# Masked softmax on one core: batch 5 and batch 0 exchange their places in the order of work

## The chip, the core and the metric

The kernel runs on one core of a Trainium2 chip. The metric is the device time of one execution in microseconds (us). Three executions of the kernel before took 156.1, 156.47 and 156.1 us, so the median is 156.1 us.

## What is computed

The input `x` holds 16 batches of 8 heads, each 256 by 256 in float32, and `lengths` holds one length for each batch. In every row only the first `length` columns count: they go through a softmax, and the other columns of the output are zero.

```python
for b in range(batch):
    length = lengths[b]
    masked = x[b, :, :, :length].copy()
    masked = masked - np.max(masked, axis=-1, keepdims=True)
    exp_masked = np.exp(masked)
    result[b, :, :, :length] = exp_masked / np.sum(exp_masked, axis=-1, keepdims=True)
```

The inputs come from a fixed draw. The lengths of batches 0 to 15 are 188, 233, 229, 243, 195, 252, 165, 210, 222, 180, 209, 157, 159, 199, 214 and 248.

## The kernel before, in words

One batch is a tile of 128 partitions by 16 rows by 256 columns, 2 MiB. The buffer `xt` has eight slots of that size, and the batch at position p of the order of work lies in slot p % 8. Before the change position p holds batch p. In what follows L4 is the load at position 4, S4 the store at position 4, and so on.

**Loads.** The first four positions are loaded whole (all 256 columns) by SyncE's queue, lines 128 to 132, the first of them in two halves. The other twelve come from GpSimd's queue, in the loop at line 178. For each it reads the length and takes the branch of `pick` (line 146) whose width is the smallest of 160, 168, ..., 240, 256 that holds the length; the DMA at line 152 then moves only so many columns of each row. The slots that are first filled in this way were set to zero beyond column 160 beforehand (line 174). In the pass for position p the loop waits until L(p-2) has landed (line 183), and until S(p-8) has landed where a slot is used again (line 184). So at most two of these loads are under way. The chip works on two DMA queues at once: q1 holds all that SyncE issues (the first loads, and every store), q0 holds GpSimd's loads.

**Stores.** SyncE issues them in the order of positions (lines 134 to 143), always whole rows, since the output has zeros beyond the length. Store 0 goes in one piece, positions 1 to 7 in a half and two quarters (called a, b and c below), 8 to 12 and 15 in two halves, 13 and 14 in one piece. Each piece waits until its division is done (line 138), and the first piece of S(p) also until S(p-2) has landed (line 140).

**Compute.** VectorE clips the right half of a batch to its length (line 222: `mask`), ScalarE takes the exponentials with the row sums (line 329), in two halves of a batch, and VectorE takes reciprocals and multiplies, half by half (lines 243 and 246: `divide`). From position 4 on VectorE's order is: first half of `divide(p)`, `mask(p + 1)`, second half of `divide(p)`. Ahead of that, `mask(4)` stands before both halves of `divide(3)`. A `mask` waits for its load. Behind the last division a few small instructions look whether a plain softmax with the row maximum would have to be done again; it is not done for this input.

Of the kernel before, what the change touches and what calls it, by code (L numbers as in the profile page):

```python
# [17 lines left out]
POOL = mybir.EngineType.Pool  # L18
# [3 lines left out]
def kernel(  # L22
# [6 lines left out]
    nc = tc.nc  # L29
    P = nc.NUM_PARTITIONS  # L30

    batch, heads, seq_q, seq_k = x.shape
# [6 lines left out]
    x_f = x.rearrange("b h q k -> b (h q) k").rearrange("b (p t) k -> b p t k", p=P)  # L39
    out_f = out.rearrange("b h q k -> b (h q) k").rearrange("b (p t) k -> b p t k", p=P)  # L40

    slots = 8
    ahead = 4
    assert slots - ahead == 4 and batch % slots == 0

    widths = list(range(160, 248, 8))
    low = widths[0]
# [3 lines left out]
    def parts(b):  # L51


        if b == 0:
            cuts = [0, nt]
        elif b < 8:
            cuts = [0, half, half + quarter, nt]
        elif b < 13 or b == batch - 1:
            cuts = [0, half, nt]
        else:  # L60
            cuts = [0, nt]
        return [slice(i, j) for i, j in zip(cuts, cuts[1:])]
# [3 lines left out]
    xt = pool.tile([P, slots, nt, seq_k], F32, name="xt")  # L66
    word64 = pool.tile([1, batch], mybir.dt.int64, name="word64")
    word = word64.bitcast(I32)
# [3 lines left out]
    len_s = pool.tile([P, batch], F32, name="len_s")  # L72
# [20 lines left out]
    with tc.tile_critical(no_gpsimd_drain=True):  # L93
# [4 lines left out]
        s_ld = [sem(f"s_ld{k}") for k in range(ahead + 1)]  # L98
# [19 lines left out]
        def length(engine, at):  # L118

            return nc.values_load(  # L120
                at,
                engines=[engine],
                skip_runtime_bounds_check_because="compared with constants, never an address",
            )
# [2 lines left out]
        nc.scalar.dma_start(out=word64, in_=lengths[None, :]).then_inc(s_word, 16)  # L127
        for h in range(2):
            s = slice(h * half, (h + 1) * half)
            nc.sync.dma_start(out=xt[:, 0, s], in_=x_f[0, :, s]).then_inc(s_ld[h], 16)  # L130
        for b in range(1, ahead):
            nc.sync.dma_start(out=xt[:, b], in_=x_f[b]).then_inc(s_ld[b + 1], 16)  # L132

        nc.sync.wait_ge(s_exp, 3)
        for b in range(batch):
            s_b = s_st[b % 2]
            for s in parts(b):
                nc.sync.wait_ge(s_out, 2 * b + (s.stop - 1) // half + 1)
                if b >= 2 and s.start == 0:
                    nc.sync.wait_ge(s_b, 64 * (b // 2 + 1))  # L140
                nc.sync.dma_start(  # L141
                    out=out_f[b, :, s, :], in_=xt[:, b % slots, s, :]
                ).then_inc(s_b, 16 * ((s.stop - s.start) // quarter))
        nc.sync.wait_ge(s_st[0], 64 * (batch // 2 + 1))

        def pick(v, n, slot, par, ws):

            if len(ws) == 1:  # L150
                w = ws[0]
                nc.gpsimd.dma_start(  # L152
                    out=xt[:, slot, :, :w], in_=x_n[:, n, :, :w]
                ).then_inc(s_sw[par], 16)
                return
            m = (len(ws) - 1) // 2
            with nc.gpsimd.If(v <= ws[m]):  # L157
                pick(v, n, slot, par, ws[: m + 1])
            with nc.gpsimd.Else():
                pick(v, n, slot, par, ws[m + 1 :])  # L160

        x_n = x_f.rearrange("b p t c -> p b t c")
        x_g = x_f.rearrange("b p t c -> p b (t c)")
# [14 lines left out]
        with nc.Fori(0, (batch - ahead) // 2, 1, engines=[POOL]) as q:  # L178
            for par in range(2):
                n = 2 * q + (ahead + par)  # L180
                v_len = length(POOL, word[0:1, bass.ds(2 * n, 1)])
                with nc.gpsimd.If(q >= 1):
                    nc.gpsimd.wait_ge(s_sw[par], 16 * q)
                    nc.gpsimd.wait_ge(s_st[par], 64 * q)
                pick(v_len, bass.ds(n, 1), bass.ds(n % slots, 1), par, widths + [seq_k])


        nc.tensor.wait_ge(s_ones, 2)
# [6 lines left out]
        v = 0  # L195

        def step(ins):
# [8 lines left out]
                out=down, in0=iota_i, scalar1=0.5, scalar2=-big, op0=ALU.add, op1=ALU.mult  # L206
# [7 lines left out]
                out=len_s, in0=len_f, scalar1=big, scalar2=None, op0=ALU.mult  # L214
# [4 lines left out]
        def clip(b, s, lo, hi):  # L219

            t = xt[:, b % slots, s, lo:hi]
            return nc.vector.scalar_tensor_tensor(  # L222
                out=t,
                in0=down[:, None, lo:hi].to_broadcast([P, s.stop - s.start, hi - lo]),
                scalar=len_s[:, b : b + 1],
                in1=t,
                op0=ALU.add,
                op1=ALU.min,
            )

        def mask(b, s):
            if b == 0:
                nc.vector.wait_ge(s_ld[s.start // half], 16)
            elif b < ahead:
                nc.vector.wait_ge(s_ld[b + 1], 16)
            else:
                nc.vector.wait_ge(s_sw[b % 2], 16 * ((b - ahead) // 2 + 1))
            clip(b, s, mid, seq_k).then_inc(s_min, 1)
# [41 lines left out]
        for k, (_, _, edge, op) in enumerate(checks):  # L280
            nc.vector.tensor_scalar(  # L281
                out=bad[:, k : k + 1],
# [13 lines left out]
        with nc.vector.Else():  # L296
            with nc.Fori(0, batch, 1, engines=[DVE]) as i:
                nc.vector.wait_ge(g_ld, 16 * i + 16)
                nc.vector.scalar_tensor_tensor(
                    out=g_t,  # L300
                    in0=down[:, None, :].to_broadcast([P, nt, seq_k]),
                    scalar=len_s[:, bass.ds(i, 1)],
# [6 lines left out]
                    out=neg_max, in_=g_t, op=ALU.max, axis=AX, negate=True  # L309
# [5 lines left out]
                    out=g_t,  # L315
# [25 lines left out]
        with nc.scalar.If(a_redo >= 1):  # L341
            for par in range(2):
                nc.scalar.wait_ge(s_st[par], 64 * (batch // 2 + 1))
            with nc.Fori(0, batch, 1, engines=[ACT]) as i:
                nc.scalar.dma_start(out=g_t, in_=x_g[:, bass.ds(i, 1)]).then_inc(g_ld, 16)
                nc.scalar.wait_ge(g_v, 3 * i + 2)
                with nc.Fori(0, nt, 1, engines=[ACT]) as t:
                    e = g_t[:, bass.ds(t, 1), :]
                    nc.scalar.activation(
                        out=e,  # L350
                        in_=e,
# [41 lines left out]
```

## Time and profile before

| what | value |
|---|---|
| median of the runs | 156.1 us |
| the profiled execution | 156.7 us, of which the span below is 155.1 us |
| VectorE busy | 117.0 us, 75% of the span |
| ScalarE busy | 105.2 us, 68% |
| GpSimd busy | 19.1 us, 12% |
| TensorE busy | 0.3 us |
| moved by DMA | 62.09 MB, mean 400 GB/s |
| queue q1 (SyncE's loads and all stores) | 41.95 MB, 65.7% of the time of 16 DMA engines |
| queue q0 (GpSimd's loads) | 20.12 MB, 32.0% of it |

The profile shows one execution. The span is what the profiler covers of it; 1.6 us of the execution lie around it. Times inside the span are counted from its start. There are 16 DMA engines, each working on packets from both queues; a share of 1 means that all 16 are busy. An engine's "idle before" names what the idle time ended with.

### The profile page before, as it was taken

Reading aid. Unit: us, or ns where it says so; the run is one execution under the profiler, and the core shown is the slowest. Engines: PE = TensorE matmul, PEld = TensorE weight load, DVE = VectorE, ACT = ScalarE, POOL = GpSimd, SP = SyncE. Lnnn points to the kernel's source line nnn. Section 1 sums busy time; section 2 is a strip of 40 time slices with the busy share of each in tenths; the row PEclk is TensorE's granted clock in tenths of the full one; section 3 lists DMA queues with packets and bytes.
Section 4 is the critical chain, followed back from the end, with each engine's and each line's share of the span. In section 5 each row is a group of like instructions: output and inputs, shape, how many; then the busy total and the mean of one; then the engine's idle time right before and its main releaser. Section 6 shows DMA issues by size and latency. Waiting matters only on the chain.

```text
span 155.1 us, 1298 instructions
## 1 busy us (share of the span) xinstructions
PE 0.3 (0%) x2; PEld 0.2 (0%) x2; DVE 117.0 (75%) x91; ACT 105.2 (68%) x514; POOL 19.1 (12%) x26
## 2 busy tenths in 40 slices
PE   0000000000000000000000000000000000000000
PEld 0000000000000000000000000000000000000000
DVE  1349999953999696969889696969679629796810
ACT  3096799992692959688795949595966906959200
POOL 4910031000220110202020020202001000000000
DMA  4999999999999999999999999999999999999991
GB/s 118 425 446 427 431 363 421 400 408 443 411 405 392 413 411 419 412 418 411 401 424 404 418 410 410 409 419 417 418 417 419 419 443 427 418 444 427 423 423 53
DMA packets 9989, 62.09 MB, mean 400 GB/s; under 512 B 850, under 2 KB 946, under 8 KB 6274
## 3 DMA queue, kind: packets, MB, share of 16 engines
q1 hardware_dynamic: 5904, 41.95, 65.7%
q0 software_dynamic: 4080, 20.12, 32.0%
q14 instruction: 3, 0.02, 0.0%
q10 hardware_dynamic: 2, 0.00, 0.0%
HBM read 28.51 MB, written 33.55 MB: 400 GB/s over the span
## 4 chain that ended last, share of the span: by engine, by line
DMA 55%; DVE 22%; ACT 7%; issue 6%; ACTq 2%; SPq 1%; POOLq 1%; PE 0%
DMA xt<-in_x_dram 34%; DMA out_dram<-xt 21%; DVE xt L246 12%; DVE xt L222 9%; ACT xt L329 7%; ACTq L329 2%; DVE inv_sum L243 1%; SPq L130 1%; DVE ends L278 0%; SPq L141 0%; POOLq L120 0%; ACTq L335 0%; SPq L132 0%; POOLq L157 0%; POOLq L152 0%
## 5 line engine op out<-in xcount | busy, mean ns | idle before, releaser
L329 ACT ACTIVATE xt<-xt (+1 forms) x256 | 102.3, 401 | 37.5 <-DVE xt L222 37.5
L246 DVE TENSOR_TENSOR xt<-xt,inv_sum 128x2048 f32<-128x2048 f32 x32 | 73.4, 2292 | 1.1
L222 DVE SCALAR_TENSOR_TENSOR xt<-down,len_s,xt 128x2048 f32<-128x2048 f32 (+1 forms) x17 | 37.8, 2222 | 13.4 <-DMA xt<-in_x_dram 13.2
L329 ACT ACTIVATION_READ_ACCUMULATOR xt<-xt (+1 forms) x256 | 47.8, 187 | 0.0
L152 POOL DMA_DIRECT2D xt<-in_x_dram x12 | 12.8, 1066 | 96.0 <-DMA out_dram<-xt 58.9
L243 DVE RECIPROCAL inv_sum<-row_sum 128x8 f32<-128x8 f32 x32 | 6.4, 199 | 14.3 <-ACT xt L329 14.3
L174 POOL MEMSET xt<- 128x1536 f32 x4 | 5.3, 1392 | 1.1 <-DVE len_s L213 1.1
L322 ACT ACT_TABLE_LOAD x1 | 1.3, 1283 | 1.6 <-SPq L93 1.6
L205 DVE TENSOR_SCALAR down<-iota_i 128x256 f32<-128x256 int32 x1 | 0.3, 302 | 1.6 <-POOL iota_i L165 1.6
L278 DVE TENSOR_REDUCE ends<-row_sum 128x1 f32<-128x256 f32 x2 | 0.7, 409 | 0.0
L192 PE MATMUL count<-bad,ones_c 128*1 128x3 bf16 x1 | 0.2, 165 | 145.2 <-DVE bad L281 145.2
L210 DVE CAST len_b<-word 1x16 bf16<-1x16 int32 x1 | 0.2, 162 | 0.4 <-DMA word<-in_lengths_dram 0.4
L213 DVE TENSOR_SCALAR len_s<-len_f 128x16 f32<-128x16 f32 x1 | 0.2, 175 | 0.4 <-PE len_f L190 0.4
L165 POOL IOTA iota_i<- 128x256 int32 x1 | 0.3, 332 | 0.6 <-SPq L93 0.6
L289 DVE TENSOR_REDUCE redo<-count 1x1 f32<-1x3 f32 x1 | 0.1, 148 | 0.3 <-PE count L192 0.3
L281 DVE TENSOR_SCALAR bad<-ends 128x1 bf16<-128x1 f32 x3 | 0.3, 150 | 0.0
L171 POOL MEMSET seed<- 1x1 f32 x2 | 0.2, 228 | 0.0
L192 PEld LDWEIGHTS count<-bad,ones_c 128*1 128x1 bf16 x1 | 0.1, 79 | 145.3 <-DVE bad L281 145.3
L322 ACT ACTIVATE warm<-const-float32-0.0 128x1 f32<-128x1 f32 x1 | 0.2, 203 | 0.0
L168 POOL MEMSET ones<- 1x128 bf16 x1 | 0.2, 195 | 0.0
L190 PE MATMUL len_f<-len_b,ones 1*128 1x16 bf16 x1 | 0.2, 168 | 2.6 <-DVE len_b L210 2.6
L278 DVE TENSOR_REDUCE ends<-len_s 128x1 f32<-128x16 f32 x1 | 0.2, 158 | 0.0
(7 smaller groups left out, 0.6 us busy)
## 6 DMA issues: line engine op xcount, KB each, us to landing
out_dram<-xt SPq DMA_DIRECT2D x19, 1024.0 KB
out_dram<-xt SPq DMA_DIRECT2D x14, 512.0 KB
xt<-in_x_dram SPq DMA_DIRECT2D x3, 2048.0 KB, 16.2
out_dram<-xt SPq DMA_DIRECT2D x3, 2048.0 KB
xt<-in_x_dram POOLq DMA_DIRECT2D x3, 1728.0 KB, 16.8
xt<-in_x_dram POOLq DMA_DIRECT2D x2, 2048.0 KB, 18.5
xt<-in_x_dram POOLq DMA_DIRECT2D x2, 1600.0 KB, 17.0
xt<-in_x_dram POOLq DMA_DIRECT2D x2, 1280.0 KB, 15.0
```

The source lines that it names most:

```text
L130: nc.sync.dma_start(out=xt[:, 0, s], in_=x_f[0, :, s]).then_inc(s_ld[h], 16)
L152: nc.gpsimd.dma_start(out=xt[:, slot, :, :w], in_=x_n[:, n, :, :w]).then_inc(s_sw[par], 16)
L165: nc.gpsimd.iota(iota_i, pattern=[[1, seq_k]], base=0, channel_multiplier=0).then_inc(s_iota, 1)
L174: nc.gpsimd.memset(xt[:, b, :, low:], 0.0).then_inc(s_fill, 1)
L192: nc.tensor.matmul(count, lhsT=ones_c, rhs=bad, start=True, stop=True).then_inc(s_count, 1)
L205: nc.vector.tensor_scalar(out=down, in0=iota_i, scalar1=0.5, scalar2=-big, op0=ALU.add, op1=ALU.mult)
L222: return nc.vector.scalar_tensor_tensor(out=t, in0=down[:, None, lo:hi].to_broadcast([P, s.stop - s.start, hi - lo]), scalar=len_s[:, b : ...
L243: step(nc.vector.reciprocal(out=inv_sum[:, b, s], in_=row_sum[:, b, s]))
L246: nc.vector.tensor_tensor(out=t, in0=t, in1=inv_sum[:, b, s, None].to_broadcast([P, half, seq_k]), op=ALU.mult,).then_inc(s_out, 1)
L278: step(nc.vector.tensor_reduce(out=ends[:, k : k + 1], in_=values, op=op, axis=AX))
L322: nc.scalar.activation(out=warm, in_=nc.const_aps.tensor(0.0, (P, 1), F32), func=EXP)
L329: ins = nc.scalar.activation(out=e, in_=e, func=EXP, accum_out=sum_h[:, i, j])
```

## The change

A table `batch_of` says which batch stands at a position: batch 5 at position 0, batch 0 at position 5, every other batch at its own number. Position 0 is loaded whole by SyncE, as before, but with the data of batch 5. Position 5 is loaded by GpSimd, as before, but with batch 0, whose width is 192 where that of batch 5 was 256. The stores go to the addresses of the batches at their positions and keep their sizes, since these go by the position. In GpSimd's loop the batch number for the odd positions is computed in registers: q = 0 gives batch 0, later q give 2q + 5. `mask` takes the length of the batch at its position; slots, semaphores and the order of the engines' instructions are as before.

```diff
+    def batch_of(pos):
+        return {0: 5, 5: 0}.get(pos, pos)
...
-            nc.sync.dma_start(out=xt[:, 0, s], in_=x_f[0, :, s]).then_inc(s_ld[h], 16)
+            nc.sync.dma_start(out=xt[:, 0, s], in_=x_f[batch_of(0), :, s]).then_inc(s_ld[h], 16)
         for b in range(1, ahead):
-            nc.sync.dma_start(out=xt[:, b], in_=x_f[b]).then_inc(s_ld[b + 1], 16)
+            nc.sync.dma_start(out=xt[:, b], in_=x_f[batch_of(b)]).then_inc(s_ld[b + 1], 16)
...
-                    out=out_f[b, :, s, :], in_=xt[:, b % slots, s, :]
+                    out=out_f[batch_of(b), :, s, :], in_=xt[:, b % slots, s, :]
...
                 n = 2 * q + (ahead + par)
-                v_len = length(POOL, word[0:1, bass.ds(2 * n, 1)])
+                b = 2 * q + (q + 7) // 8 * 5 if par else n
+                v_len = length(POOL, word[0:1, bass.ds(2 * b, 1)])
                 with nc.gpsimd.If(q >= 1):
                     nc.gpsimd.wait_ge(s_sw[par], 16 * q)
                     nc.gpsimd.wait_ge(s_st[par], 64 * q)
-                pick(v_len, bass.ds(n, 1), bass.ds(n % slots, 1), par, widths + [seq_k])
+                pick(v_len, bass.ds(b, 1), bass.ds(n % slots, 1), par, widths + [seq_k])
...
-                scalar=len_s[:, b : b + 1],
+                scalar=len_s[:, batch_of(b) : batch_of(b) + 1],
```

More of the change, by code (lines that the diff above doesn't have):

```diff
@@ L43 @@
     ahead = 4
-    assert slots - ahead == 4 and batch % slots == 0
+    assert slots - ahead == 4 and batch == 2 * slots
+    def batch_of(pos):
+        return {0: 5, 5: 0}.get(pos, pos)
     widths = list(range(160, 248, 8))
@@ L141, with pick @@
                 nc.sync.dma_start(
-                    out=out_f[b, :, s, :], in_=xt[:, b % slots, s, :]
+                    out=out_f[batch_of(b), :, s, :], in_=xt[:, b % slots, s, :]
                 ).then_inc(s_b, 16 * ((s.stop - s.start) // quarter))
         nc.sync.wait_ge(s_st[0], 64 * (batch // 2 + 1))
-        def pick(v, n, slot, par, ws):
+        def pick(v, b, slot, par, ws):
             if len(ws) == 1:
@@ L152, in pick @@
                 nc.gpsimd.dma_start(
-                    out=xt[:, slot, :, :w], in_=x_n[:, n, :, :w]
+                    out=xt[:, slot, :, :w], in_=x_n[:, b, :, :w]
                 ).then_inc(s_sw[par], 16)
@@ L157, in pick @@
             with nc.gpsimd.If(v <= ws[m]):
-                pick(v, n, slot, par, ws[: m + 1])
+                pick(v, b, slot, par, ws[: m + 1])
             with nc.gpsimd.Else():
-                pick(v, n, slot, par, ws[m + 1 :])
+                pick(v, b, slot, par, ws[m + 1 :])
         x_n = x_f.rearrange("b p t c -> p b t c")
```

## Prediction

> **What bounds the kernel now.** I read the page's slices first, then the stretches, then the order in time of VectorE, GpSimd and SyncE, and last the trace's single DMA packets.
>
> The slices: the DMA engines are full from the second slice to the last but one, no compute engine is.
>
> ```profile
> DVE  1349999953999696969889696969679629796810
> ACT  3096799992692959688795949595966906959200
> ...
> DMA  4999999999999999999999999999999999999991
> ```
>
> The stretches (start:end, length, busy time of PE, PEld, DVE, ACT, POOL with counts, clock, DMA share, GB/s) say the same near the end:
>
> ```profile
> 127.00:140.00 13.00, 0.00 (x0) 0.00 (x0) 11.75 (x8) 8.63 (x43) 0.00 (x0) 1.00 1.02 432
> 140.00:147.30 7.30, 0.00 (x0) 0.00 (x0) 5.41 (x7) 4.37 (x22) 0.00 (x0) 1.00 0.99 421
> 147.30:152.00 4.70, 0.17 (x1) 0.08 (x1) 0.78 (x6) 0.00 (x0) 0.00 (x0) 1.00 0.90 382
> ```
>
> So bytes bound it, but a second limit lies close by. VectorE in order of time (start, length; idle before it in brackets):
>
> ```profile
> 115.16 2.35 DVE L222 SCALAR_TENSOR_TENSOR xt<-down,len_s,xt 128x2048 f32<-128x2048 f32 x1 [0.89 <-DMA xt<-in_x_dram]
> ...
> 126.88 2.35 DVE L222 SCALAR_TENSOR_TENSOR xt<-down,len_s,xt 128x2048 f32<-128x2048 f32 x1 [3.25 <-DMA xt<-in_x_dram]
> ...
> 137.76 2.29 DVE L246 TENSOR_TENSOR xt<-xt,inv_sum 128x2048 f32<-128x2048 f32 x1
> ```
>
> mask(13) and mask(14) wait for their loads. From mask(14) at 126.88 to the end of the second half of divide(14), 137.76 + 2.29 = 140.05, nothing waits for a DMA: 13.2 us of compute hang on L14. SyncE issues S14 at 140.08, at once. Behind it come 2 + 1 + 1 MiB. By the packet records the slowest of the 16 engines ends the last store at 153.4; S14 and S15 are 8 packets of 16 KB and 16 of 8 KB for it, 8 x 0.613 + 16 x 0.317 = 10.0 us at the records' mean durations, so it was free for S14 at 143.4. So S14 comes about 2 us before the slowest engine needs it. **If L14 lands over 2 us later, that engine idles, and the end moves.**
>
> **How the two queues share.** Counted from the packet records, per DMA engine: every whole or part store is 8 packets (of 16, 8 or 4 KB, for whole, half, quarter); a whole load is 8 of 16 KB; a narrow load is cut into packets of several rows, under 5 KB: 22 for width 200, 19 for 168, 26 for 216. With both queues filled the engines alternate: from 104 to 112 us 272 packets of 4800 B (q0) and 244 of 8 KB (q1), from 116 to 124 288 of 4320 B and 257, from 36 to 40 87 of 16 KB and 90 of 4 KB. q0 gets 1.0 to 1.15 packets per store packet whatever their sizes. The Trainium skill (DMA: Bandwidth & Descriptors, Queues, rings and completion order) says that an engine goes round its queues packet by packet; the counts agree. Beside quarters (4 KB) a whole load thus takes four fifths of the bandwidth; a narrow one takes little over half, and beside halves (8 KB) two fifths.
>
> **The change part by part.**
>
> 1. *Bytes.* Position 0 stays 2 MiB. L5 goes from 8 x 16 KB packets per engine, 613 ns each: 4.90 us, to 128 rows of 768 B per engine; six to a packet as for 736 and 800 B rows, so 21 of 4608 B and a short one. Between 177 ns (4416 B) and 191 (4800 B) I take 184: 21 x 0.184 + 0.06 = 3.92 us. **-0.98 us** of all engines. The bounds are -0.8 and -1.1 (22 x 0.191, and 21 x 0.177 + 0.06). The Trainium skill (same page, Anatomy of one DMA) prices moving data at bytes / 436e9; for 0.524 MB that is an estimate of 1.20 us. By it the term would be -1.2; the rows decide.
>
> 2. *Registers.* GpSimd gets one extra register operation for each odd length and one in each odd branch. Its register rows are 29 ns (move) and 110 to 130 (fused). The length is read before the waits, so hidden; the one in the branch costs odd loads 0 to 0.13 us at issue. Writing L5's descriptors takes about 1.15 us in place of 0.56:
>
> ```profile
> 20.93 1.30 POOL L152 DMA_DIRECT2D xt<-in_x_dram  x1 [12.53 <-issue]
> 24.14 0.56 POOL L152 DMA_DIRECT2D xt<-in_x_dram  x1 [1.92 <-issue]
> 38.80 1.16 POOL L152 DMA_DIRECT2D xt<-in_x_dram  x1 [14.10 <-issue]
> 44.98 1.15 POOL L152 DMA_DIRECT2D xt<-in_x_dram  x1 [5.02 <-DMA out_dram<-xt]
> ```
>
> L4 keeps q0 filled to 36.3, so this costs 0 (0.6 without that cover). The addresses of S0 and S5 and the scalars of two masks change, no size: 0.
>
> 3. *L5 gets slower though smaller.* Before, its 8 packets per engine met 8 store packets (S1c): 36.3 to 42.2, landed 43.55. Now 22 packets meet about 20: 8 of S1c, 8 of S2a (8 KB), 4 of S2b. A q0 packet with a 4 KB partner takes 0.32 (4320 B) to 0.36 us (4800 B), with an 8 KB one 0.44 to 0.47; 13 x 0.34 + 9 x 0.46 = 8.5 us. It lands at about 46.0, **2.5 us later**; mask(5) started at 47.04 without waiting, so 1 us remains there.
>
> 4. *The gate of L7.* L6 was issued at 38.80, 1.4 us after L4 landed (37.43), and its first packets came at 43.5, 4.7 us behind the issue; from 42.2 to 43.5 and more q0 was empty and some 4 store packets per engine ran alone. Now L5 covers that. But L7 waits for L5: 46.0 + 1.4 + 4.7 = 52.1 for its first packet, up to 52.9, where it was 50.5 to 51.3: +1.6, with some 0.1 of point 2; I take **+1.8**. Behind this wait on GpSimd stands only the pass of L8, issued at 53.58 before and gated by L6. The engines do not idle, so what L7 loses the stores gain: (1.8 + 0.98) / 0.317 us (an 8 KB packet) = 9 store packets ahead.
>
> 5. *It stays.* Thereafter the queues alternate as before, and stores have slack to run ahead: the second half of divide(8) is done at 85.35, S8 moves from 97. So L10 (landed 89.01, S7a next) still sees stores 8 x 0.317 + 0.2 = 2.7 ahead, less 0.98: +1.7. L12 is gated by L10: issued at 90.52, first packets 95.2, when L11 had ended at 94.5: so +1.7 there too. From there L12, L13, L14 have 19, 22 and 26 packets, now all beside 8 KB pieces: 19 x 0.4475 + 22 x 0.47 + 26 x 0.444 = 30.4 us, before 29.7 (95.2 to the ends around 124.9), because L12 had 4 KB partners at first: +0.7. **L14 lands 2.4 us later**, at about 129.2. Bounds: 0.3 if the stores ahead at the time of L10 are 4 KB ones, 4.0 if q0 gets no more than one packet per store packet and a new hole opens at L12.
>
> 6. *The tail.* S14 is issued at 140.08 + 2.4 = 142.5. From issue to first packet the trace has 1.0 us (first load, 1.14 to 2.15) and 2.5 (S13, 134.17 to 136.7, behind others); nearer the empty queue I take 1.5, so 144.0. The slowest engine is free at 143.4 - 0.98 = 142.4. It idles 1.6 us: the end moves by -0.98 + 1.6 = **+0.6 us**. S15's halves (issued 144.11 and 146.95, so 149.4 and first packets by 150.9) then come behind 144.0 + 4.9 + 2.5 = 151.4 and are hidden. Against the profiled execution's own 156.7 that is 157.3; the runs' median is 0.6 below that execution, so **156.7 us**.
>
> In short: end = the larger of -0.98 (bytes bind) and L14's delay minus 1.8 (compute after L14 binds).
>
> **Rivals.**
>
> *The bytes win.* If L14 is late by under 0.8 us, all -0.98 is kept: 155.1; up to 1.3, some of it: 155.6. For it: full DMA in all slices, and q0 drawing more than one packet per store packet; stores that get ahead may run dry at S12 or S13, which wait for their division, and then q0 has the engines alone. Against it: S8 to S11 have 10 us and more of such slack, and the gates of L7 and L12 do not depend on bytes.
>
> *They cancel.* L14 late by 1.3 to 2.3: within 0.5 us of 156.1, 0.3%, about what a measurement of this kernel can tell from no change.
>
> *The loads fall further behind* (slower still). With one to one, 22 packets meet 22, and if L6 ends before L7's gate and L11 before L12's by more, 3 to 5 more store packets go first (0.317 each): L14 +3.4 to 4.0, end +1.6 to 2.2: 157.7 to 158.3. It decides from 2.3 us of delay on, the forecast being its mild form.
>
> *The change does not do what it says*: batch 0 falls in another branch than 192. Then q0 would not drop by 0.52 MB; with 256 columns the time stays at 156.1.
>
> **How the numbers follow.** Forecast (L14 late by 2.3 to 3.3, +0.5 to +1.5): 0.39. Further behind: 0.09. Cancel: 0.22, and 0.02 for a change that does nothing. Bytes win: 0.28. So slower by over 0.3% 0.48, within 0.24, faster 0.28. The range from 155.1 (bytes alone) to 157.8 leaves out the last of "further behind" and what is faster than the bytes: about 2 in 10.
>
> **What would show it.** Right: moved bytes 61.57 MB; L5 lands near 46 and not at 43.5; L7 issued near 47.5 (44.98 before); mask(14) starts near 129 after a wait over 4 us; the DMA share dips below 0.95 between 140 and 145. Wrong: L5 lands at 43 or earlier (no alternation by packets); mask(14) at 127 or before (the lead of the stores was lost again); no dip in the tail although mask(14) is late (more slack there than 1.8 us).

## The result, and the profile after

The changed kernel takes 157.91 us (median of six executions, 157.38 to 158.78); the kernel before, run beside it, 156.25 us (155.68 to 156.59). The ratio is 1.0111, with a 95% interval of 1.0074 to 1.0148: **slower by 1.1%, 1.66 us**. The prediction was slower too, but by 0.6 us, 156.7 us in a range up to 157.8; the time lies just outside. The profiled execution after took 157.94 us with a span of 156.3 us.

The slices of the page, as before the change:

```profile
DVE  1349999944999696877969677997966656697780
ACT  3096899991792959588494947869591970978800
...
DMA  4999999999999999999999999999999999992994
GB/s 115 428 438 436 432 361 415 406 406 415 393 380 412 398 419 410 414 419 406 418 403 416 415 409 418 411 417 419 415 416 419 418 437 423 409 455 109 419 403 203
DMA packets 10213, 61.57 MB, mean 394 GB/s; under 512 B 850, under 2 KB 962, under 8 KB 6626
```

0.52 MB less is moved, as the change says. But the row of the DMA engines has a hole in the fourth slice from the end, where it had none. The stretches around it (columns as in the prediction):

```profile
127.00:140.00 13.00, 0.00 (x0) 0.00 (x0) 8.52 (x7) 7.33 (x37) 0.00 (x0) 1.00 1.03 436
140.00:142.50 2.50, 0.00 (x0) 0.00 (x0) 2.46 (x3) 1.04 (x5) 0.00 (x0) 1.00 0.46 197
142.50:144.50 2.00, 0.00 (x0) 0.00 (x0) 1.14 (x1) 2.00 (x11) 0.00 (x0) 1.00 0.00 0
144.50:152.00 7.50, 0.17 (x1) 0.08 (x1) 6.15 (x11) 3.45 (x18) 0.00 (x0) 1.00 1.02 428
```

For two microseconds not one data packet starts. S13 has gone out, and S14 waits for the division. VectorE in order of time says why the division is late:

```profile
118.74 2.35 DVE L227 SCALAR_TENSOR_TENSOR xt<-down,len_s,xt 128x2048 f32<-128x2048 f32 x1 [1.50 <-DMA xt<-in_x_dram]
...
130.47 2.35 DVE L227 SCALAR_TENSOR_TENSOR xt<-down,len_s,xt 128x2048 f32<-128x2048 f32 x1 [3.26 <-DMA xt<-in_x_dram]
...
141.35 2.29 DVE L251 TENSOR_TENSOR xt<-xt,inv_sum 128x2048 f32<-128x2048 f32 x1
```

mask(14) starts at 130.47, 3.6 us later than before, because L14 lands so late. The 13.2 us of compute behind it are the same (141.35 + 2.29 = 143.64), S14 is issued at 143.67, and its first packet moves at 144.51. GpSimd's issues show where the lateness began:

```profile
24.53 1.15 POOL L156 DMA_DIRECT2D xt<-in_x_dram  x1 [2.36 <-issue]
38.82 1.15 POOL L156 DMA_DIRECT2D xt<-in_x_dram  x1 [13.13 <-issue]
47.61 1.15 POOL L156 DMA_DIRECT2D xt<-in_x_dram  x1 [7.64 <-issue]
```

L6 is issued when it was before, L5 0.4 us later but long before L4 ends (36.1); L7, which waits for L5, at 47.61 in place of 44.98, since L5 with fewer bytes landed at 46.10 in place of 43.55.

How far the stores get ahead can be counted in the packet records: store packets sent (q1, per engine, from the start, the first loads included) when the median engine ends or starts a load.

| when | before | after | ahead |
|---|---|---|---|
| L4 ends | 64.9 | 64.7 | 0 |
| L5 ends | 73.2 | 85.1 | 11.9 |
| L6 starts | 79.2 | 88.4 | 9.2 |
| L6 ends | 95.5 | 107.2 | 11.7 |
| L7 ends | 120.2 | 132.6 | 12.4 |
| L10 ends | 191.0 | 203.8 | 12.8 |
| L12 starts | 212.8 | 225.9 | 13.1 |
| L14 ends | 273.2 | 286.4 | 13.2 |

The stores win the lead beside L5 and L6 and keep it for 80 us.

### The profile page after: what moved, and what is told of

The parts are those of the page before. It is cut to its first block, busy times and chain, and to the rows that moved or that the text cites. A ratio compares the mean times of both kernels' runs of the same rounds, so it can differ in the third digit from the quotient of the medians.

```text
span 156.3 us, 1312 instructions
## 1 busy us (share of the span) xinstructions
PE 0.3 (0%) x2; PEld 0.2 (0%) x2; DVE 117.2 (75%) x91; ACT 105.2 (67%) x514; POOL 19.7 (13%) x26
## 4 chain that ended last, share of the span: by engine, by line
DMA 76%; DVE 7%; issue 6%; ACT 4%; POOLq 2%; ACTq 1%; SPq 1%; PE 0%
DMA xt<-in_x_dram 76%; ACT xt L334 4%; DVE xt L227 3%; DVE xt L251 3%; ACTq L334 1%; POOLq L161 1%; POOLq L156 1%; SPq L134 1%; DVE ends L283 0%; POOLq L124 0%; DVE inv_sum L248 0%; SPq L136 0%; DVE bad L286 0%; POOLq L187 0%; ACTq L340 0%
## 5 line engine op out<-in xcount | busy, mean ns | idle before, releaser
L156 POOL DMA_DIRECT2D xt<-in_x_dram x12 | 13.4, 1116 | 99.0 <-issue 99.0
```

The lines of the kernel that those rows point to most:

```text
L156: nc.gpsimd.dma_start(out=xt[:, slot, :, :w], in_=x_n[:, b, :, :w]).then_inc(s_sw[par], 16)
```

## The experiments

The theory: the DMA engines take turns between the queues packet by packet; 22 thin packets in L5's place let 13 more store packets pass before L14 is in, L14 is 3.6 us late, and S14 and what follows come after the engines have run dry. Rival A: something else of the change costs the time, the registers and longer descriptor writing on GpSimd, or the addresses. Rival B: bytes alone count, and the rest is scatter. Each kernel was timed beside the kernel before on the same chip, and each ratio is to those runs.

### The exchange without the narrow load, and a wider narrow load

In the first of two kernels position 5 is loaded whole. The number added to the length is 64 at position 5 and zero later.

```diff
+                if par:
+                    v_len = v_len + (1 - (q + 7) // 8) * 64
                 pick(v_len, bass.ds(b, 1), bass.ds(n % slots, 1), par, widths + [seq_k])
```

> The changed kernel, but position 5 (batch 0) is loaded with all 256 columns: 8 packets of 16 KB per DMA engine instead of 22 thin ones. The exchange, the registers and the addresses stay. Theory (the engines alternate packet by packet, so 22 thin packets let the stores get about 13 packets ahead, L14 comes late, and the tail idles): L5 lands near 43.5 us as before the change, mask(14) starts near 127, no idle in the tail, time about 156.2 us, ratio to before 1.000. Rival A (something else of the change costs it: GpSimd's registers and its longer descriptor writing, the other addresses): as the changed kernel, about 157.9. Rival B (bytes alone, the rest scatter): 156.2 too, so the next kernel is what tells B apart.

Measured: 156.12 us beside 156.08, ratio 1.0009 (0.9998 to 1.0021). The loss is gone. L5 lands at 43.31, mask(14) starts at 126.85, and the stretches of the tail are full:

```profile
126.85 2.35 DVE L229 SCALAR_TENSOR_TENSOR xt<-down,len_s,xt 128x2048 f32<-128x2048 f32 x1 [3.25 <-DMA xt<-in_x_dram]
...
140.00:142.50 2.50, 0.00 (x0) 0.00 (x0) 1.31 (x3) 2.50 (x13) 0.00 (x0) 1.00 1.00 426
142.50:144.50 2.00, 0.00 (x0) 0.00 (x0) 1.34 (x2) 1.83 (x10) 0.00 (x0) 1.00 1.01 434
```

The exchange, its registers and its addresses cost nothing that can be measured. With the whole width the writing of L5's descriptors is short again as well (0.56 us and not 1.15), so this run alone does not clear that part of rival A; the kernel with four loads under way, below, keeps the 1.15 us and takes 155.91 us. Rival A falls. In the second kernel the added number is 50, so batch 0 is loaded 240 columns wide: nearly the bytes of the kernel before, in 26 thin packets.

```diff
-                    v_len = v_len + (1 - (q + 7) // 8) * 64
+                    v_len = v_len + (1 - (q + 7) // 8) * 50
```

> The changed kernel, but position 5 is loaded 240 columns wide: 128 rows of 960 B per engine, 5 to a packet, 26 packets, 1.97 MB, 0.13 MB less than the kernel before moved. Theory: 4 packets more than in the changed kernel, so the stores get 16 to 17 packets ahead of where they are in the kernel before; L5's own work is 4.95 us as before, so L14 lands 16.5 x 0.317 = 5.2 us later than before (about 132), and the end follows with about 2.4 us of slack: +2.8 us, 159 us (158.3 to 160). Rival B (bytes): 156.1. Rival A (something else of the change): 157.9.

Measured: 159.11 us, ratio 1.0203 (1.018 to 1.0226). L5 lands at 47.79, 4.2 us later than before. VectorE's two waits late in the run, and the tail:

```profile
119.57 2.35 DVE L229 SCALAR_TENSOR_TENSOR xt<-down,len_s,xt 128x2048 f32<-128x2048 f32 x1 [1.41 <-DMA xt<-in_x_dram]
131.29 2.35 DVE L229 SCALAR_TENSOR_TENSOR xt<-down,len_s,xt 128x2048 f32<-128x2048 f32 x1 [3.26 <-DMA xt<-in_x_dram]
```

```profile
140.00:142.50 2.50, 0.00 (x0) 0.00 (x0) 2.47 (x3) 0.61 (x3) 0.00 (x0) 1.00 0.86 367
142.50:145.50 3.00, 0.00 (x0) 0.00 (x0) 1.97 (x1) 3.00 (x17) 0.00 (x0) 1.00 0.22 93
```

0.13 MB less than the kernel before, and 3 us slower: rival B falls. Loads of almost the same bytes differ by three microseconds by how they are cut. L14 was less late than expected (131.3, not 132): the lead at its end was 286.7 - 273.2 = 13.5 packets where 16 to 17 were expected. It was 137.9 - 120.2 = 17.7 at the end of L7 and shrank from there on. The packet records show where: between L9 and L10, and between L11 and L12, only about one store packet per engine passes here, where about 3 and 4 pass in the kernel before and in the changed kernel. No run tries why L10 and L12 follow so closely here.

### The tail

S14 goes out in two halves, the first of which waits only for the first half of its division.

```diff
-        elif b < 13 or b == batch - 1:
+        elif b != 13:
             cuts = [0, half, nt]
```

> The changed kernel, but S14 goes out in two halves, so its first half can be issued when the first half of divide(14) is done, near 139, and not at 143.7. Theory (the engines idle from 142.6 to 144.5 because S14 comes late): that idle time goes; then the halves of S15 bind, whose last is issued when all division is done (150.5) and needs 0.85 + 2.5 us: the end comes 0.6 to 0.9 us earlier than in the changed kernel, about 157.1 us. If the tail's idle time were not on the path: no change, 157.9.

Measured: 157.42 us, ratio 1.0088 (1.0066 to 1.011); 0.5 us less than the changed kernel, 157.91. But the interval of that one's ratio (1.0074 to 1.0148) holds this one's, so the gain is not shown. The hole did not close but was broken up: by the packet records the engines run low before each of the last stores (around 137, 145, 148.5 to 149, and 152). The stretch with one of these holes:

```profile
147.00:149.50 2.50, 0.00 (x0) 0.00 (x0) 1.81 (x3) 1.91 (x10) 0.00 (x0) 1.00 0.57 233
```

In this execution L14 also landed later than in the changed kernel (131.40 against 130.44), so the run does not single out the tail. It does show that S14 in one piece is not the whole of the loss: all that follows L14 is late, and the idle time comes back elsewhere.

### Three ways to bring the loads forward

If the lateness of L14 is the cause, whatever cures it must cure the time, at either end of the run. One: S8 to S12 in a half and two quarters, so the late loads meet 4 KB packets.

```diff
-        elif b < 8:
+        elif b < 13:
             cuts = [0, half, half + quarter, nt]
```

> The changed kernel, but S8 to S12 go out in a half and two quarters, like S1 to S7, so L12 to L14 meet 4 KB packets for two thirds of theirs. Theory: a thin load packet takes 0.32 to 0.36 us beside a 4 KB packet and 0.44 to 0.47 beside an 8 KB one, so L12 to L14 take about 25 us in place of 30; mask(14) no longer waits for its load or much less (start near 126 or before), the engines do not idle in the tail, and the end is set by the bytes: 0.98 us less than before plus some 0.2 us for more small packets, 155.4 us. Rivals A and B, in which the alternation plays no part: 157.9 to 158.1.

Measured: 156.56 us, ratio 1.0024 (1.0012 to 1.0036). mask(14) starts with no wait, and the engines' share stays at 0.94 to 1.03 from 140 to 150.5; the theory holds for that:

```profile
125.96 2.34 DVE L227 SCALAR_TENSOR_TENSOR xt<-down,len_s,xt 128x2048 f32<-128x2048 f32 x1
```

But the time is not the expected 155.4. The same edit in the kernel before is the control:

> The kernel before the change, with S8 to S12 in a half and two quarters: the control of the quarters. Its engines never idle, so loads that come earlier win nothing. Theory (the end is set by the packets' time): 640 store packets of 8 KB become 1280 of 4 KB, 640 x (2 x 163 - 317 ns) / 16 = +0.36 us, 156.4 us. The difference to the changed kernel with quarters (156.56) is then what the change is worth when the loads are not late: -0.98 us if only the bytes count (then this run would be at 157.5), near 0 if the engines' saving is used up by longer packets (156.4 to 156.6). Rival: quarters help the kernel before as well (155.5 or less).

Measured: 156.67 us, ratio 1.0036 (1.0025 to 1.0047). So the quarters cost 0.6 us by themselves (0.36%), where 0.36 us was expected and the packet records show 0.42 us more per engine (151.54 against 151.12), and with them the change is worth -0.1 to -0.2 us, which the two intervals do not tell from nothing. Two: the same quarters for S11 and S12 alone.

```diff
-        elif b < 8:
+        elif b < 8 or b in (11, 12):
```

> The changed kernel with only S11 and S12 in a half and two quarters. L14 meets S11a and then the two quarters of S11: 26 load packets take 8 x 0.444 + 18 x 0.32 = 9.3 us in place of 11.1. Theory: L14 lands near 128.6, the end comes 1.8 us earlier, 156.1 us, where the engines' packets bind (with 0.15 us for the small packets). If lateness of L14 were not what sets the end: 157.9 to 158.1.

Measured: 156.19 us, ratio 1.0013 (1.0001 to 1.0025). mask(14) starts at 127.85, after a wait of 1.35 us for its load; the time is the expected one. Three: S2 and S3 in four quarters, 80 us ahead of the tail, where the lead is won.

```diff
+        elif b in (2, 3):
+            cuts = [0, quarter, half, half + quarter, nt]
         elif b < 8:
```

> The changed kernel with S2 and S3 in four quarters each, so L5 and L6 meet only 4 KB packets: the stores get ahead by the same number of packets but by fewer bytes; 8 more packets of 4 KB in each of S2 and S3 hold the stores back by 2 x 8 x 0.163 = 2.6 us. Theory (the lead that the stores win beside L5 to L7 is what makes L14 late, at the other end of the run): L14 lands near 127.8 and the end comes 1.9 us earlier, at the limit of the engines' packets, 156.0 us. If the lead were lost or won again on the way, or L14's delay came from the late positions alone: 157.9 us.

Measured: 155.76 us, ratio 0.9981 (0.9967 to 0.9994). The only waits for loads late in the run:

```profile
114.40 2.35 DVE L229 SCALAR_TENSOR_TENSOR xt<-down,len_s,xt 128x2048 f32<-128x2048 f32 x1 [0.33 <-DMA xt<-in_x_dram]
126.09 2.35 DVE L229 SCALAR_TENSOR_TENSOR xt<-down,len_s,xt 128x2048 f32<-128x2048 f32 x1 [3.22 <-DMA xt<-in_x_dram]
```

An edit that touches two stores before 60 us moves mask(14) by 4.4 us and the end by 2.1 us (2.0 by the ratios): the lead is won early and carried through. At the end of L14 the stores are 289.5 - 273.2 = 16 packets ahead, and 16 is what the finer cut of S2 and S3 adds for the same bytes, so in bytes no lead is left. This kernel has the lowest median of the study. It beats the kernel before by 0.2%, barely clear of the noise, and its interval meets that of the kernel with four loads, below.

### The gates of the loads

Up to four of GpSimd's loads may be under way, with a semaphore for each position modulo 4.

```diff
-        with nc.Fori(0, (batch - ahead) // 2, 1, engines=[POOL]) as q:
-            for par in range(2):
-                n = 2 * q + (ahead + par)
-                b = 2 * q + (q + 7) // 8 * 5 if par else n
+        with nc.Fori(0, (batch - ahead) // 4, 1, engines=[POOL]) as r:
+            for j in range(4):
+                n = 4 * r + (ahead + j)
+                b = 4 * r + (r + 3) // 4 * 5 if j == 1 else n
...
-                with nc.gpsimd.If(q >= 1):
-                    nc.gpsimd.wait_ge(s_sw[par], 16 * q)
-                    nc.gpsimd.wait_ge(s_st[par], 64 * q)
+                with nc.gpsimd.If(r >= 1):
+                    nc.gpsimd.wait_ge(s_sw[j], 16 * r)
+                    nc.gpsimd.wait_ge(s_st[j % 2], 128 * r + 64 * (j // 2))
```

> The changed kernel, but up to four of GpSimd's loads may be under way (four semaphores for them, one per position modulo 4), so L(p) waits for L(p-4) and not L(p-2). Theory with the gates as a cause: in the changed kernel a DMA engine sends 1.9, 3.0 and 4.5 store packets alone between L6 and L7, L9 and L10, L11 and L12, where 1.2 is usual; these 5.8 packets x 0.317 = 1.8 us go, L14 lands near 128.6 and the end comes 1.8 us earlier, 156.1 us. If only the number of thin packets counts and the gates do not: 157.9 us.

Measured: 155.91 us, ratio 0.9992 (0.9981 to 1.0003). GpSimd issues L4 to L7 in one go:

```profile
20.83 1.31 POOL L156 DMA_DIRECT2D xt<-in_x_dram  x1 [12.44 <-issue]
24.51 1.15 POOL L156 DMA_DIRECT2D xt<-in_x_dram  x1 [2.38 <-issue]
27.13 1.15 POOL L156 DMA_DIRECT2D xt<-in_x_dram  x1 [1.47 <-issue]
30.33 1.15 POOL L156 DMA_DIRECT2D xt<-in_x_dram  x1 [2.05 <-issue]
```

L5 still takes until 44.55 (median engine) and gives the stores about the same lead (85.7 packets, 85.1 in the changed kernel); but from then on only 1.0 to 2.1 store packets pass between two loads, and at the end of L14 the lead is 275.2 - 273.2 = 2:

```profile
127.31 2.35 DVE L227 SCALAR_TENSOR_TENSOR xt<-down,len_s,xt 128x2048 f32<-128x2048 f32 x1 [3.25 <-DMA xt<-in_x_dram]
```

The thin packets make the lead, and loads that are queued ahead win it back. The kernel before was not run with four loads under way; it has holes between its loads too (6.0 store packets between L5 and L6, by the table), so it is not shown that the exchange costs nothing where both kernels have none.

### What the bytes are worth once the loads are on time

Two last kernels: the kernel before with S2 and S3 in quarters, and the changed kernel with both cures.

> The kernel before the change with S2 and S3 in four quarters each: the control of the run before last with these quarters (155.76 us). There the loads come early enough already, so theory says only the packets' time counts: 256 store packets of 8 KB become 512 of 4 KB, 256 x 9 ns / 16 = +0.14 us, 156.1 us. The changed kernel with the same quarters is then 0.35 us below it: what is left of the 0.98 us by which L5 got smaller. If the full 0.98 us were to be had, this run would be at 156.7; if the quarters themselves are what gained, at 155.6.

> The changed kernel with both cures: four loads under way, and S2 and S3 in four quarters. Theory: L14 lands near 124.5 and no longer matters, the engines never idle, and the end is the time of their packets, as with the quarters alone (155.76) or 0.2 us under it: 155.5 to 155.8 us. If L14 still set the end in the run with the quarters alone: 154.5 or less.

Measured: 156.53 us, ratio 1.0029 (1.0017 to 1.004), and 156.43 us, ratio 1.0018 (1.0004 to 1.0031). The first says that the quarters of S2 and S3 cost the kernel before 0.5 us, and that with them the change is worth 155.76 - 156.53 = -0.8 us (ratios 0.9981 and 1.0029, intervals apart), near the -0.98 of the bytes. The other pair of kernels, with S8 to S12 in quarters, gave only -0.1 to -0.2 us, so what the bytes are worth depends on the rest of the order and is not one number. The run with both cures does not fit: L14 lands at 121.84, the packets' time is the least of all (150.4 us per engine), and its median is still 0.7 us above that with the quarters alone. Its profiled execution took 155.76 us, the lowest of its twelve, so the trace does not hold the time that the median lost. The expectation for both was missed, and what sets the last half microsecond in kernels whose loads come very early stays open.

## Why the prediction was right in direction and wrong in size

- **What bounds it** (bytes, and L14's compute close behind): right. The condition "if L14 lands over 2 us later, the end moves" is what happened: L14's mask 3.6 us later, the hole in the tail, the end after it.
- **Point 1, -0.98 us of packets**: the rows were right (4608 B took 184 ns), but the packets' time per engine fell only from 151.12 to 150.77 us, since store packets got longer: 8 KB ones 320 ns on average in place of 317, 4 KB ones 165 in place of 163. So of the 0.98 us some 0.35 was kept; that packets would keep their durations was taken without a row for it.
- **Point 2, registers**: right, nothing (156.12 us with the registers and the addresses in place; the longer descriptor writing, 1.15 us, is in the kernel with four loads, at 155.91 us).
- **Point 3, L5 slower though smaller**: right to 0.1 us, and in its working: landed 46.10, predicted 46.0, with 20.4 store packets beside its 22, where about 20 were predicted.
- **Point 4, the gate of L7 and the lead of 9 packets**: here the sum failed. The 9 packets were to be the whole lead, from L7 on; 9.2 was the lead when L6 started. Then L6 itself met 18.8 store packets with its 19, where I had let it keep its share (16.3 before), so it ended at 51.9 to 54.0 (50.0 to 51.3 before). Why it lost its share is open: it stood beside S3a's 8 KB pieces now, but elsewhere such pieces left q0 1.1 packets for one (272 to 244). L7's gate (first packets 52.7 to 53.5, against 52.1 to 52.9 predicted) opened at about the time when L6 ended and was not the worse of the two.
- **Point 5, "it stays"**: right in kind. But 12 to 13 packets stayed, not 9: L10 landed 3.0 us later (91.98), not 1.7, and L14 **3.6 us later, not 2.4**. The 0.7 us for L12 to L14 was right (0.6). What L10 meets is the mis-sized term. By the packet records up to its end, 7.6 store packets of 8 KB and 5.3 of 4 KB per engine more than before had gone, 3.3 us at the durations of before, where 2.7 was taken. The longer store packets of point 1, which the sum put at nothing, add 0.5 us, and the loads take 1.1 us less. Together that is 2.7 us; the median engine ended L10 2.6 us later, and the last engine, on which the landing waits, 3.0.
- **Point 6, the tail**: S14's first packet came at 144.51, only 0.5 us after the predicted 144.0 although L14 was 1.2 us later than predicted, since 0.84 us passed from its issue and not 1.5. The last packet of S13 ended at 142.9 (142.4 predicted), so that engine idled the predicted 1.6 us, by luck: both ends of the idle time came 0.5 us late. The end of the last store moved from 153.4 to 154.6, 1.2 us and not 0.6. The medians moved by 1.66, because the profiled execution of before lay 0.45 us above its median (its slowest engine ended at 153.4; with position 5 whole, in an execution of 155.99 us, at 152.7) and that of after, 157.94, at its median. The prediction had taken 0.6 us off for this, from 157.3 to 156.7, and in the changed kernel there was nothing to take off. So the miss of 1.2 us is 0.6 in the trace and 0.6 in this last step; that L14 was missed by 1.2 us too is a coincidence, and so is the good fit of "L14's delay minus 1.8" with the medians.
- **The rivals**: "the loads fall further behind" named this outcome and priced it at 157.7 to 158.3. Its one-to-one pairing showed at L6, not at L5, where it had put it. It had 0.09 and should have had more, since the rows gave 1.0 to 1.15 load packets per store packet and only the upper half was used.
- **A slip without effect**: the smaller bound of point 1 is 4.90 - 22 x 0.191 = 0.7 us, not 0.8.

The Trainium skill (DMA: Bandwidth & Descriptors, Queues, rings and completion order) says that an engine takes its queues in turn, packet by packet; the counts agree (L5's 22 packets beside 20.4 store packets, L6's 19 beside 18.8). The Trainium skill (same page, SWDGE vs HWDGE vs iDMA) puts a packet at no more than 4096 B preferably; here it was 16 KB for whole loads and 4.3 to 4.8 KB for narrow ones. The 16 KB packets are what L5 gave up.

## What to carry to other kernels

When two DMA queues share the engines, as here, count packets beside bytes: a load that is cut thinner can land later although it is smaller (L5, 0.52 MB less, 2.55 us later), and the other queue keeps the lead until something lets it be won back (here 13 packets for 80 us). Before trimming bytes from a transfer, look at what size its packets will have, what stands beside it in the other queue, and which wait near the end its lateness would reach. If the trim is wanted, pay for it where the lead is won (here smaller store pieces at the same time, or more loads under way), and time the same cure on the kernel before.

## What was not expected of the hardware

- Between 40 and 45 us, beside L5's thin packets, the 8 KB store packets took 355 ns on average (single ones up to 892), against 311 in the same stretch before and 313 in most others. The kernel with 240 columns shows it too (364), that with L5 whole does not (310). By itself it is 0.2 of the 0.6 us that point 1 lost (76 packets, 42 ns each, over 16 engines); from 30 to 50 us as a whole, 8 KB packets took 335 ns against 313 before and 4 KB packets 169 against 163, and that is nearly all of it. The cause is not known.
- From GpSimd's issue to a load's first packet 4.7 us passed while the engines were busy (38.80 to 43.5), from SyncE's issue with all engines idle 0.84 us (143.67 to 144.51). Where the issue came too late for the load to be queued behind the one ahead of it, 3 to 8 store packets per engine passed (6.0 before L6 in the kernel before, 8 before L7 with 240 columns); queued ahead, 1 to 2.
- Stores cut into more pieces cost more than their packets in the two controls: 0.5 us with S2 and S3 in quarters, where the packets' time per engine did not rise (151.10 us against 151.12), and 0.6 us with S8 to S12, where it rose by 0.42. In the profiles with more pieces 1.8 to 2.2 us lie between the last packet and the end of the span, in the others 1.5 to 1.7; whether this makes the difference was not tried.
